# Pair evictions placed ahead of splits, values fetched into their own tiles, an embedding product in two portions, and priority for the first values' weights, in a two-layer mLSTM and retention trunk

## The chip, the cores and the metric

The kernel runs on one core of a Trainium2 chip. Its engines are named as in the profile: PE (TensorE, matrix products; PEld is its loading of weights), DVE (VectorE), ACT (ScalarE), POOL (GpSimd) and SP (SyncE, which here only issues transfers). Each engine works through its own instructions in a fixed order, and an instruction that waits holds up everything behind it on that engine. The metric is device time in microseconds (us); less is better.

## The reference, cut to what matters

The computation is a trunk of two layers over 512 positions of width 1024, in float32. Each layer has an mLSTM branch, a retention branch of four heads, a merge, a feed-forward part of width 4096, and a gated embedding.

```python
for i in range(DEPTH):                       # 2 layers
    h = rmsnorm(x, norm1_g[i])
    z = h @ w_in[i] + b_in[i]                # mLSTM q k v o i f, retention q k v g, two gates
    _, _, mv, mo, mi, mf, rq, rk, rv, rg, gm, gr = split_cols(z)
    qk = jax.nn.silu(causal_conv(z[..., :2 * M_QK], conv_w[i], conv_b[i]))
    hm = mlstm_chunkwise(mq, mk, mv, mi, log_sigmoid(mf))
    y_m = sigmoid(mo) * head_layernorm(hm, m_norm_g[i], M_HEADS)
    rq4, rk4 = rope(rq), rope(rk) * R_DK ** -0.5
    hr = retention_chunkwise(rq4, rk4, rv, log_gamma)      # 4 heads, dk 256, dv 512
    y_r = silu(rg) * head_layernorm(hr, r_norm_g[i], R_HEADS)
    merged = sigmoid(gm) * (y_m @ w_bm[i]) + sigmoid(gr) * (y_r @ w_br[i])
    x = x + merged @ w_out[i]
    h2 = rmsnorm(x, norm2_g[i])
    x = x + square(relu(h2 @ w_ff1[i] + b_ff1[i])) @ w_ff2[i] + b_ff2[i]
    h3 = rmsnorm(x, norm3_g[i])
    x = x + sigmoid(h3 @ w_pe_gate[i]) * (p[i] @ w_pe[i])   # the embedding
return rmsnorm(x, final_g)
```

## The kernel before, in words

**Precision.** Every float32 operand is kept as two tiles, a rounded "hi" and the rest "lo". The function `split` makes them: ACT copies the source into hi (L286), DVE subtracts hi from the source into lo (L287). A product is then three matmuls, hi by hi, hi by lo and lo by hi (L442 to L444 for plain products, L491 to L493 for pairs, L534 to L536 for wide products, L746 to L748 for the first values). So each weight passes ACT and DVE before PE can use it.

**Weights.** All weights are streamed once. SP loads them in the order of a list of units into a few raw buffers `wr`; `prep_next` splits the next piece into `wh` and `wl`, two pieces ahead of the product that uses it. In names such as wh53_C, 53 is the unit and C the piece. A unit of kind T8 or V is one 128x1024 piece of eight blocks; PE is the embedding's weight, in two units.

**Pairs.** Two column tiles of a 1024-deep product form a PAIR, computed by Strassen's method in Winograd's form: seven products P1 to P7 of 12 matmuls (256 wide) where eight would be needed. Its weights are four pieces: A serves P1 and P5, B serves P6 and P2, C serves P3 and P7, D serves P4. Sums of weights for A and C are made in memory by DMAs that POOL issues (L331, tiles s*t1 and s*t3, 1 MB each, paced by the matmuls); two further sums are made on DVE (L421, L424). PE runs P1, P5, then the P4 that the pair before left over (`later`, `flush`), then P6, P2, P3, P7, and leaves its own P4. In the profile a product is told by its PSUM tile and its weights, such as l0r2o1a with wh_A. P1, P6, P7 and P4 add up in one PSUM bank ("a"), P5 and P3 in another ("c"), P2 stands alone ("b"). So each later product in a bank must wait until the earlier sum has been read out ("evicted"). In `pair_tiles` P1 (L548), P5 (L550), P6 (L554) and P4 (L560) are read out by ACT, P2 (L552), P3 (L556) and P7 (L558) by DVE.

**Retention heads.** For head h of layer i the names are l{i}r{h}. `r_qk` makes queries and keys (pairs brq and brk with rotary work on DVE), `r_scores` the scores s and p, `r_attend` the product with the values (tile l{i}r{h}a, read out by ACT L783 as num) and its normalisation: statistics on DVE (L791, L792), two small instructions on POOL (L1086, L1087, tile hv), and a scaling on DVE (L797). `r_out` multiplies by the gate (pairs o0 and o1 of the head). Values are computed for two heads at once: head 0 or 2 is split at once into the value tiles vh and vl, head 1 or 3 is written to memory by POOL (L1166). `rv_load` brings the latter back: POOL issues four transfers of 256 KB into temporary tiles vr (L1197), and each tile is split into vh and vl. There is one set of value tiles per branch, so these may be overwritten only when the head before has been read.

**Feed-forward and embedding.** hid tiles (hh, hl) come from ff1; `ff2(b, p)` are pairs named l{i}o{b}{p}, whose evictions add straight into x on DVE (L1400). The last four are o30 to o33. The embedding's product l{i}pe takes two units of 24 matmuls of 512 columns and reads neither x nor hid; ACT copies its eight tiles (L1450). After o33 the third normalisation n3 feeds the gate product l{i}pg.

**What sets the order.** A scheduler lays out each engine's order when the program is built: it takes ready instructions by priority, which is the order of the code, and its own estimate of when inputs are ready. `tc.high_priority(offset)` makes the instructions inside count as if they were written that many places earlier. On the chip the order is then fixed.

Of the kernel before, what the change touches and what calls it, by code (L numbers as in the profile page):

```python
# [53 lines left out]
LOOK = 2  # L54
WARM = 11
# [95 lines left out]
def unit_list(i):  # L151
# [77 lines left out]
    u.append(("PE", 0))  # L229
    u.append(("PE", 1))  # L230
    pairs(ff_order()[1])
# [4 lines left out]
def build(ctx, tc, ins, out):  # L236
# [153 lines left out]
    def prep_next():  # L390
# [15 lines left out]
        if gates:  # L406
            z = out_[0]
            gp.memset(z.bitcast(F32), 0.0)
            z = z.rearrange("p (k g c) -> p k g c", g=4, c=32)
            split(r[:, 0:64].rearrange("p (k g c) -> p k g c", g=2, c=H), z[:, :, 0:2, 0:H], z[:, :, 2:4, 0:H])  # L410
        elif x == 0:
            for c in halves(n):
                in_order("prep", *split(r[:, c], *[a[:, c] for a in out_]))
        else:
            in_order("prep", *split(r[:, :w], *out_))
# [124 lines left out]

    def pair_tiles(name, act, consume, y=None):
# [4 lines left out]
        def done(x, o):  # L546
            if x == "P1":
# [3 lines left out]
            elif x == "P2":  # L551
                ve.tensor_tensor(y[0][:, b], o, y[0][:, b], OP.add)  # L552
            elif x == "P6":
                ac.activation(y[1][:, b], o, AF.Copy)  # L554
            elif x == "P3":
                ve.tensor_tensor(y[1][:, b], o, y[1][:, b], OP.add)  # L556
            elif x == "P7":
                ve.tensor_tensor(y[1][:, a], o, y[1][:, a], OP.add)  # L558
            else:
                ac.activation(y[0][:, a], o, AF.Copy)  # L560
                consume(y)
# [357 lines left out]
    for i in range(L):  # L919
# [272 lines left out]
        def rv_load(h):  # L1192

            v = value_tiles(f"l{i}r{h}")
            for j in range(NT):
                t = tmp(f"l{i}r{h}vr{j}")
                gp.dma_start(t, rv_dram[i, h // 2, j])  # L1197
                split(t, v[0][j][:, :T], v[1][j][:, :T])
            return v

# [81 lines left out]
        num = r_attend(0, pt, vv)  # L1282
        gs = {}
        r_gates(0, 0, gs)
        vv = rv_load(1)
        pt = r_scores(1, qk)
        yr = acts(cur["br"], f"l{i}yr0")
# [8 lines left out]
        num = r_attend(2, pt, vv)  # L1296
        qk = r_qk(3)
# [5 lines left out]
        vv = rv_load(3)  # L1303
        pt = r_scores(3, qk)
        yr = acts(cur["br"], f"l{i}yr1")
# [137 lines left out]
        for u in range(2):  # L1443
            _, wh, wl = unit("PE")
            for c in range(4):
# [4 lines left out]
                ac.activation(pe[:, 4 * u + c, :], o, AF.Copy)  # L1450
        for _, b, p in rest:
            ff2(b, p)
        flush()
# [216 lines left out]
```

## Time and profile before

| | us |
|---|---|
| median of 3 runs | 2349.16 |
| lowest and highest run | 2348.27, 2350.61 |
| the profiled execution's own time | 2347.49 |
| span of that execution in the trace | 2345.8 |
| PE busy in the span | 2320.2 |
| DVE busy | 1722.9 |
| ACT busy | 1218.9 |
| POOL busy | 245.7 |

The trace belongs to one execution; its times of day count from the start of the span. Matmuls overlap each other, so an instruction's own length (0.28 to 0.39 us) is longer than the distance to the next one (0.12 us at 256 columns, 0.23 us at 512). In timeline rows the columns are start, length, engine, line, operation, output and inputs; the square bracket says how long the engine was idle just before and what ended it. In rows of waits the numbers are the sum, the number of waits and the longest.

### The profile page before, as it was taken

What the parts mean: (1) busy time and instruction counts of PE and PEld (TensorE: products, weight loads), DVE (VectorE), ACT (ScalarE), POOL (GpSimd) and SP (SyncE); (2) the same over time, 40 slices, a digit from 0 to 9 for tenths busy, and PEclk for the clock granted to TensorE, in tenths of its full rate; (3) what the DMA queues carried; (4) which work ended last, traced back from release to release, by engine and by line L of the source; (5) the groups of instructions that cost most, each with busy time, mean ns of one, the idle gap of its engine ahead of it and who ended that gap; (6) DMA issues with size and microseconds to landing.
All of it is one profiled execution on the core that took longest, in us unless ns stands there. A gap on an engine that the chain in (4) does not pass through costs nothing. (4 is left out here: it accounts for less than half of the span.)

```text
span 2345.8 us, 35261 instructions
## 1 busy us (share of the span) xinstructions
PE 2320.2 (99%) x13660; PEld 2056.2 (88%) x13660; DVE 1722.9 (73%) x2658; ACT 1218.9 (52%) x1768; POOL 245.7 (10%) x369
## 2 busy tenths in 40 slices
PE   9999999999999999999999999999999999999998
PEld 7888899898898898899888888998989988998997
DVE  7878767895675577677878787778958656776785
ACT  6656444553554445446557564454536445445454
POOL 3111101100102100000321110000000020000012
PEclk9999999999999999999999999999999999999999
DMA  5666676667578667676775645434343542433431
GB/s 201 187 180 172 218 229 170 205 189 202 168 230 269 195 198 189 199 219 181 206 221 169 182 124 186 136 126 158 108 158 104 166 153 96 130 108 98 132 117 59
DMA packets 146631, 394.89 MB, mean 168 GB/s; under 512 B 15376, under 2 KB 18832, under 8 KB 146464
## 3 DMA queue, kind: packets, MB, share of 16 engines
q1 hardware_dynamic: 99952, 247.77, 32.0%
q0 software_dynamic: 31104, 117.45, 20.4%
q10 hardware_dynamic: 15408, 27.43, 3.3%
q8 instruction: 107, 1.75, 0.3%
q14 instruction: 60, 0.49, 0.1%
HBM read 373.71 MB, written 123.73 MB: 212 GB/s over the span
## 5 line engine op out<-in xcount | busy, mean ns | idle before, releaser
L286 ACT ACTIVATE wh<-wr 128x1024 fp32r<-128x1024 f32 (+1 forms) x223 | 232.2, 1044 | 276.5 <-issue 69.6
L287 DVE TENSOR_TENSOR wl<-wr,wh 128x1024 fp32r<-128x1024 f32 (+1 forms) x221 | 271.9, 1232 | 77.7 <-ACT wh L286 77.5
L286 ACT ACTIVATE wh_B<-wr 128x1024 fp32r<-128x1024 f32 x100 | 105.9, 1059 | 159.2 <-PE l0f L443 8.5
L287 DVE TENSOR_TENSOR wl_B<-wr,wh_B 128x1024 fp32r<-128x1024 f32 x100 | 121.9, 1219 | 32.5 <-ACT wh_B L286 32.3
L286 ACT ACTIVATE wh_D<-wr 128x512 fp32r<-128x512 f32 x76 | 48.0, 632 | 124.9 <-DVE wr L424 65.4
L286 ACT ACTIVATE wh_C<-wr 128x1024 fp32r<-128x1024 f32 x76 | 80.2, 1056 | 61.3 <-issue 9.2
L286 ACT ACTIVATE wh_A<-wr 128x1024 fp32r<-128x1024 f32 x76 | 79.9, 1052 | 54.7 <-PE l1f L443 9.0
L287 DVE TENSOR_TENSOR wl_C<-wr,wh_C 128x1024 fp32r<-128x1024 f32 x76 | 94.3, 1240 | 18.7 <-ACT wh_C L286 18.5
L287 DVE TENSOR_TENSOR wl_A<-wr,wh_A 128x1024 fp32r<-128x1024 f32 x76 | 92.7, 1220 | 17.3 <-ACT wh_A L286 17.3
L442 PE MATMUL l1f<-l1n2h,wh 128*128 128x512 f32 x256 | 99.8, 390 | 0.0
L442 PE MATMUL l0f<-l0n2h,wh 128*128 128x512 f32 x256 | 99.8, 390 | 0.0
L444 PE MATMUL l0f<-l0n2h,wl 128*128 128x512 f32 x256 | 99.7, 389 | 0.0
L444 PE MATMUL l1f<-l1n2h,wl 128*128 128x512 f32 x256 | 99.7, 389 | 0.0
L443 PE MATMUL l1f<-l1n2l,wh 128*128 128x512 f32 x256 | 99.6, 389 | 0.0
L443 PE MATMUL l0f<-l0n2l,wh 128*128 128x512 f32 x256 | 99.6, 389 | 0.0
L287 DVE TENSOR_TENSOR wl_D<-wr,wh_D 128x512 fp32r<-128x512 f32 x76 | 52.4, 689 | 33.2 <-ACT wh_D L286 31.7
L421 DVE TENSOR_TENSOR wr<-wr,wr 128x512 f32<-128x512 f32 x76 | 52.1, 686 | 14.6 <-DMA wr<-wpairs 13.1
L444 PEld LDWEIGHTS l0f<-l0n2h,wl 128*128 128x128 f32 x256 | 48.0, 188 | 10.2
L444 PEld LDWEIGHTS l1f<-l1n2h,wl 128*128 128x128 f32 x256 | 48.1, 188 | 10.1
L443 PEld LDWEIGHTS l1f<-l1n2l,wh 128*128 128x128 f32 x256 | 48.1, 188 | 9.8
L442 PEld LDWEIGHTS l0f<-l0n2h,wh 128*128 128x128 f32 x256 | 48.1, 188 | 9.8
L442 PEld LDWEIGHTS l1f<-l1n2h,wh 128*128 128x128 f32 x256 | 48.1, 188 | 9.7
(5625 smaller groups left out, 8357.9 us busy)
## 6 DMA issues: line engine op xcount, KB each, us to landing
wr<-wstream SPq DMA_DIRECT2D x219, 512.0 KB, 4.2
wr<-wpairs SPq DMA_DIRECT2D x228, 256.0 KB, 2.8
wr<-wwide SPq DMA_DIRECT2D x24, 512.0 KB, 4.0
s0t<-wwide POOLq DMA_DIRECT2D x5, 1024.0 KB, 7.8
s4t<-wwide POOLq DMA_DIRECT2D x5, 1024.0 KB, 9.0
s12t<-wwide POOLq DMA_DIRECT2D x5, 1024.0 KB, 8.1
s16t<-wwide POOLq DMA_DIRECT2D x5, 1024.0 KB, 8.5
s1t<-wpairs POOLq DMA_DIRECT2D x4, 1024.0 KB, 6.7
```

The costliest lines, as they stand in the source:

```text
L286: a = ac.activation(hi_ap, src, AF.Copy)
L287: return a, ve.tensor_sub(lo_ap, src, hi_ap.bitcast(F32))
L421: ve.tensor_tensor(raws[n, "B"][:, Q:], kept.pop((n, "A"))[:, Q:], r[:, :Q], OP.add)
L442: te.matmul(o, sh, mh, start=first, stop=False)
L443: te.matmul(o, sh, ml, start=False, stop=False)
L444: cur["mm"] = te.matmul(o, sl, mh, start=False, stop=last)
```

## The change

It has four parts.

1. In `pair_tiles` every eviction is issued under a priority of 250 places ahead, so the scheduler puts it ahead of splits that were written before it. What follows the last eviction (`consume`) keeps its priority.
2. `rv_load` is taken apart. `rv_fetch` issues the four transfers straight into the lo value tiles, right after the attend of the head before; `rv_split`, after the scores, lets ACT copy lo into hi and DVE subtract hi from lo in place. The four temporary tiles vr are gone.
3. The embedding's two units are parted: unit 0 stays before the last ff2 pairs, unit 1 comes after them, and the P4 that o33 leaves is run in the middle of unit 1 (after its second tile). SP's order of loads moves with it.
4. The splits of the first values' weights (units of kind V below 10, so layer 0 alone) get the priority of 250 places.

```diff
+AHEAD = 250
@@ list of units
     pairs(ff_order()[0])
     u.append(("PE", 0))
+    pairs(ff_order()[1])
     u.append(("PE", 1))
-    pairs(ff_order()[1])
     full("w_pe_gate")
@@ prep_next
         elif x == 0:
-            for c in halves(n):
-                in_order("prep", *split(r[:, c], *[a[:, c] for a in out_]))
+            with tc.high_priority(AHEAD if n < 10 and units[n][0] == "V" else 0):
+                for c in halves(n):
+                    in_order("prep", *split(r[:, c], *[a[:, c] for a in out_]))
@@ pair_tiles
+    def ahead():
+
+        return tc.high_priority(AHEAD)
+
...
         def done(x, o):
+            with ahead():
+                evict(x, o)
+            if x == "P4":
+                consume(y)
+
+        def evict(x, o):
             if x == "P1":
...
             else:
                 ac.activation(y[0][:, a], o, AF.Copy)
-                consume(y)
@@ values of the odd heads
-        def rv_load(h):
+        def rv_fetch(h):
 
             v = value_tiles(f"l{i}r{h}")
             for j in range(NT):
-                t = tmp(f"l{i}r{h}vr{j}")
-                gp.dma_start(t, rv_dram[i, h // 2, j])
-                split(t, v[0][j][:, :T], v[1][j][:, :T])
+                gp.dma_start(v[1][j][:, :T].bitcast(F32), rv_dram[i, h // 2, j])
             return v
+
+        def rv_split(v):
+            for hi, lo in zip(*v):
+                split(lo[:, :T].bitcast(F32), hi[:, :T], lo[:, :T])
@@ the layer
         num = r_attend(0, pt, vv)
+        vv = rv_fetch(1)
         gs = {}
         r_gates(0, 0, gs)
-        vv = rv_load(1)
         pt = r_scores(1, qk)
+        rv_split(vv)
...
         num = r_attend(2, pt, vv)
+        vv = rv_fetch(3)
         qk = r_qk(3)
...
-        vv = rv_load(3)
         pt = r_scores(3, qk)
+        rv_split(vv)
@@ the embedding
-        for u in range(2):
+
+        def embed(u):
             _, wh, wl = unit("PE")
             for c in range(4):
...
                 ac.activation(pe[:, 4 * u + c, :], o, AF.Copy)
+                if c == 1:
+                    flush()
+
+        embed(0)
         for _, b, p in rest:
             ff2(b, p)
-        flush()
+        embed(1)
```

In the changed program line numbers are higher, by 1 at the top and by 10 to 16 further down: L286 and L287 become L287 and L288, L331 becomes L332, the evictions L548 to L560 become L560 to L572, L1086 becomes L1097, L1400 becomes L1415. How the order moved is shown at three places.

The first is POOL in layer 0, around the values of head 3 (l0r3). Tiles s7t to s9t are sums of weights. Before, the end of the sums for s8 and then the fetch into vr:

```order
L331 DMA s8t3_110<-wpairs 256x1024
L331 DMA s8t1_109<-wpairs 256x1024
L331 DMA s8t3_110<-wpairs 256x1024
L1197 DMA l0r3vr0_6030<-rv_spill_83 128x512
L1197 DMA l0r3vr1_6034<-rv_spill_83 128x512
L1197 DMA l0r3vr2_6038<-rv_spill_83 128x512
L1197 DMA l0r3vr3_6042<-rv_spill_83 128x512
L331 DMA s9t1_111<-wpairs 256x1024
```

In the changed program, the same fetch, now into vl:

```order
L332 DMA s7t1_107<-wpairs 256x1024
L1207 DMA l0r3vl0_5465<-rv_spill_83 128x512
L1207 DMA l0r3vl1_5466<-rv_spill_83 128x512
L1207 DMA l0r3vl2_5467<-rv_spill_83 128x512
L1207 DMA l0r3vl3_5468<-rv_spill_83 128x512
L1097 TENSOR_SCALAR l0r2hv_5454<-l0r2mv_5445 128x4
L1098 TENSOR_TENSOR l0r2hv_5454<-l0r2hv_5454,nhalf_89 128x4
L332 DMA s7t3_108<-wpairs 256x1024
```

The fetch moved past five sums of weights (the last of s7 and the four of s8), and now stands ahead of the two small instructions that the normalisation of head 2 needs.

The second is ACT in layer 0, around the first gate pair of head 0 (l0r0o0). Before, with kh the keys of head 1 and num the last read-out of head 0's attend:

```order
L783 ACTIVATE l0r0num_3984<-l0r0a3_4036 128x512
L286 ACTIVATE l0r1kh0_3733<-l0r1brku0_4003 128x512
L548 ACTIVATE l0r0o0y0_4067<-l0r0o0a_4078 128x256
L286 ACTIVATE l0r1kh1_3735<-l0r1brku1_4010 128x512
L550 ACTIVATE l0r0o0y1_4068<-l0r0o0c_4098 128x256
L554 ACTIVATE l0r0o0y1_4068<-l0r0o0a_4078 128x256
L286 ACTIVATE wh52_D_4094<-wr77_3850 128x512
L286 ACTIVATE wh53_A_4112<-wr78_3852 128x1024
L286 ACTIVATE l0r1vh0_4174<-l0r1vr0_4182 128x512
```

In the changed program:

```order
L794 ACTIVATE l0r0num_3984<-l0r0a3_4036 128x512
L287 ACTIVATE l0r1kh1_3735<-l0r1brku1_4010 128x512
L287 ACTIVATE l0r1vh0_4067<-l0r1vl0_4071 128x512
L560 ACTIVATE l0r0o0y0_4079<-l0r0o0a_4090 128x256
L287 ACTIVATE l0r1vh1_4068<-l0r1vl1_4072 128x512
L287 ACTIVATE l0r1vh2_4069<-l0r1vl2_4073 128x512
L287 ACTIVATE l0r1vh3_4070<-l0r1vl3_4074 128x512
L562 ACTIVATE l0r0o0y1_4080<-l0r0o0c_4110 128x256
L566 ACTIVATE l0r0o0y1_4080<-l0r0o0a_4090 128x256
L287 ACTIVATE wh52_D_4106<-wr77_3850 128x512
```

The four copies of head 1's values moved from behind three evictions (P1, P5, P6) to places between the attend and the evictions of P1 and P5.

The third is DVE near the start, around the split of unit 8, the last but one of the first values' weights; the rows between are the work on gates (lower-case g names) and on the convolution (z and cv) of mLSTM head 0. Before:

```order
L287 TENSOR_TENSOR wl7_0_580<-wr7_264,wh7_0_579 128x1024
L853 SCALAR_TENSOR_TENSOR l0glb_471<-ones_r_87,l0glf_469 4x128 x4
L855 SCALAR_TENSOR_TENSOR l0gm_476<-l0glf_469,l0gli_447 4x512
...
L979 TENSOR_TENSOR l0m00cv_495<-l0m00cv_495,l0fix_252 128x3
L978 SCALAR_TENSOR_TENSOR l0m01cv_506<-l0m01z_507,bc_84,l0m01cv_506 128x510
L287 TENSOR_TENSOR wl8_0_610<-wr8_360,wh8_0_609 128x1024
```

In the changed program:

```order
L288 TENSOR_TENSOR wl7_0_580<-wr7_264,wh7_0_579 128x1024
L857 TENSOR_TENSOR l0gd_463<-l0gd_463,l0gu_461 4x512
L858 SCALAR_TENSOR_TENSOR l0gf_446<-l0gf_446,l0gd_463 4x512
L288 TENSOR_TENSOR wl8_0_610<-wr8_360,wh8_0_609 128x1024
L864 SCALAR_TENSOR_TENSOR l0glb_471<-ones_r_87,l0glf_469 4x128 x4
```

The split of unit 8 moved past eight instructions on gates and nine of the convolution (one of each kind of row is shown, or two); those now run behind it.

## The prediction

> **What bounds the kernel now.** I read the page first, then the waits of PE, then the timeline at the waits the change touches.
>
> ```profile
> span 2345.8 us, 35261 instructions
> PE 2320.2 (99%) x13660; PEld 2056.2 (88%) x13660; DVE 1722.9 (73%) x2658; ACT 1218.9 (52%) x1768; POOL 245.7 (10%) x369
> ```
>
> PE is the bound: it is busy for all but 25.6 us, and the change removes no matmul. So it can win only what PE waits, plus what PE loses at a low clock, and it loses by any new wait of PE. The waits of PE (total, number, longest) that stand near the change:
>
> ```profile
> PE l0r2o1a L491 <- ACT wh_A L286: 3.4, 1, 3.4
> PE l1o33a L491 <- DVE l1x L1400: 1.6, 1, 1.6
> PE l0o33a L491 <- DVE l0x L1400: 1.3, 1, 1.3
> PE l0m0vp L747 <- DVE wl L287: 1.3, 1, 1.3
> PE l0r0o0a L491 <- DVE l0r0o0y L558: 1.2, 1, 1.2
> PE l1r0o0a L491 <- DVE l1r0o0y L558: 1.2, 1, 1.2
> PE l0r1brqa L491 <- DVE l0r1brqy L558: 1.0, 1, 1.0
> PE l1r2o0a L491 <- ACT l1r2o0y L548: 0.5, 1, 0.5
> PE l0r2o0a L491 <- ACT l0r2o0y L548: 0.4, 1, 0.4
> PE l1r2o1a L491 <- DVE l1r2o1y L558: 0.3, 1, 0.3
> PE l0r2o1a L491 <- DVE l0r2o1y L558: 0.2, 1, 0.2
> ```
>
> The longest is in layer 0, at the gate pairs of head 2. POOL, ACT and PE there, and the windows of the two stretches behind it and of one in layer 1 (length; busy time of PE, PEld, DVE, ACT, POOL; clock; DMA share; GB/s):
>
> ```profile
> 587.23 0.90 POOL L331 DMA_DIRECT2D s8t<-wpairs  x1 [9.98 <-DMA br_spill<-l0brs]
> 587.88 1.95 POOL L1197 DMA_DIRECT2D l0r3vr<-rv_spill  x3
> 598.58 0.63 ACT L286 ACTIVATE l0r3vh<-l0r3vr 128x512 fp32r<-128x512 f32 x1 [2.83 <-DMA l0r3vr<-rv_spill]
> 602.69 1.04 ACT L286 ACTIVATE wh_A<-wr 128x1024 fp32r<-128x1024 f32 x1
> 603.78 0.58 PE L491 MATMUL l0r2o1a<-l0xnh,wh_A 128*128 128x256 f32 x1 [3.40 <-ACT wh_A L286]
> 602.40:609.20 6.80, 5.06 (x22) 4.77 (x23) 4.96 (x11) 3.99 (x9) 0.00 (x0) 0.50 0.48 172
> 609.20:616.00 6.80, 6.80 (x59) 6.80 (x59) 3.91 (x6) 3.25 (x7) 0.00 (x0) 1.00 0.25 80
> 1563.00:1583.00 20.00, 18.79 (x137) 17.77 (x136) 18.75 (x35) 13.12 (x21) 4.02 (x6) 1.00 0.47 150
> ```
>
> POOL issued three of the four value transfers at 587.88, just behind 1 MB of weight sums. They landed so late that ACT stood idle 2.83 us for the first it came to, and the split of wh_A, behind these copies on ACT, ended at 603.73. PE waited 3.40 us and then ran at half clock for the rest of a 6.80 us stretch.
>
> **The change part by part.** *Fetch of head 3.* In the new order POOL issues it at head 2's attend, some 60 us earlier, and ACT and DVE split the values among the pairs r3brq. Nothing of it stands before wh_A any more, and PE's order there becomes regular again. In layer 0 goes 3.40, the 0.35 and 0.2 that follow it (the rows of 0.4 and 0.2) and the half clock: 5.06 us for 22 matmuls, against 6.80 / 59 = 0.115 each at full clock, is 5.06 - 2.53 = 2.5 lost; a few matmul records may be missing, so 2.4. Sum -6.35, between -3.4 (the clock's loss comes back by another wait) and -6.9. In layer 1 there was no late landing, and the two evictions waited for (0.5 and 0.3) no longer stand behind splits: -0.8, between 0 and -0.8. The cover of the moved fetch is head 3's brq and brk work; what it costs there comes below.
>
> *Embedding in two portions.* 48 matmuls of l0pe:
>
> ```profile
> L442 PE MATMUL l0pe<-l0pth,wh x16: 394/394/397, 1077.3 to 1087.6; 128*128 128x512 f32 x16
> L444 PE MATMUL l0pe<-l0pth,wl x16: 392/392/394, 1077.8 to 1088.1; 128*128 128x512 f32 x16
> 1083.55 1.23 DVE L287 TENSOR_TENSOR l0hl<-l0f33st,l0hh 128x1024 fp32r<-128x1024 f32 x1 [1.13 <-ACT l0hh L286]
> 1088.33 0.28 PE L491 MATMUL l0o30a<-l0hh,wh_A 128*128 128x256 f32 x1
> 1089.39 1.23 DVE L287 TENSOR_TENSOR wl_B<-wr,wh_B 128x1024 fp32r<-128x1024 f32 x1 [2.46 <-ACT wh_B L286]
> 1127.01 1.98 DVE L287 TENSOR_TENSOR wl<-wr,wh 128x1024 fp32r<-128x1024 f32 x1
> 1128.91 0.41 DVE L1400 TENSOR_TENSOR l0x<-l0x,l0o33a 128x256 f32<-128x256 f32 x1
> ```
>
> They start over (1088.1 - 1077.3) / 47 = 0.23 us apart. At o33 the eviction of P7 stood behind a split of the next weights on DVE (1127.01 to 1128.9), and P4 waited 1.3 us (1.6 in layer 1). Twelve embedding matmuls, 2.8 us, now lie there and hide it: -2.9 in both layers. But o30 loses 24 matmuls of cover and would start 5.5 us earlier, at 1082.8, while the last hid tile is split only until 1084.8. P1 doesn't read that part; P6 comes two products (2.8 us) later, at 1085.7, and its third matmul needs wl_B. DVE can do wl_B only after 1084.8, one eviction (0.33) and 1.2 for itself, so by 1086.3: a wait of 0.4, up to 1.0 with the L421 sum that moved ahead of the hid split. I take 0.5 a layer: -2.9 + 1.0 = -1.9, between -2.9 and 0.
>
> *Priority for the first values' weights.* wl of unit 8 moved past 17 DVE instructions:
>
> ```profile
> 50.68 1.22 DVE L287 TENSOR_TENSOR wl<-wr,wh 128x1024 fp32r<-128x1024 f32 x1
> 69.90 0.50 PE L442 MATMUL l0m0s<-l0m0qh,l0m0kh 128*128 128x512 f32 x1
> ```
>
> PE waited 1.3 us for it. Of what now runs later, PE first needs the convolution's queries and keys, at 69.90, and it reads 18 us of other products before. -1.3, between 0 (another product waits instead) and -1.4.
>
> *Evictions ahead, at r0o0.* This part meets the moved fetch of head 1 on ACT:
>
> ```profile
> L444 PE MATMUL l0r0a<-l0r0vh,l0r0pl x10: 389/389/398, 395.0 to 402.9; 128*128 128x512 f32 x10
> DMA to landing us min/median/max: 2.9/3.4/3.7
> 404.84 0.39 ACT L548 ACTIVATE l0r0o0y<-l0r0o0a 128x256 f32<-128x256 f32 x1 [0.24 <-PE l0r0o0a L493]
> 406.49 0.37 ACT L550 ACTIVATE l0r0o0y<-l0r0o0c 128x256 f32<-128x256 f32 x1
> 410.31 1.92 DVE L797 TENSOR_SCALAR l0r0num<-l0r0num,l0r0mv,l0r0hv 128x512 f32<-128x512 f32 x4 [1.26 <-POOL l0r0hv L1087]
> 415.67 0.42 DVE L558 TENSOR_TENSOR l0r0o0y<-l0r0o0a,l0r0o0y 128x256 f32<-128x256 f32 x1
> ```
>
> (The second row is the landing of l0r1vr.) The first fetch can be issued when the attend has read vl0 for the last time, about 2 us before its end at 403.2, the last one at that end. With 3.4 us to land they arrive at about 404.6 to 406.6. ACT then copies vh0, evicts P1, copies vh1 to vh3 and evicts P5: the last copy starts at about 406.9 and the eviction ends at about 407.9, where it ended at 406.9 before. PE's new order brings P3 forward (two matmuls each of P6 and P2 and three of the scores lie between), to 407.2, so P3 waits about 0.7. P7's eviction is ahead of the splits now, but on DVE still behind the scaling L797, which waits for POOL's hv. hv comes behind the four fetches, so L797 ends near 411.6, and behind it come L424, vl0 and wl_D at 0.6 each and P2's and P3's evictions at 0.33, until 414.1; P7's eviction ends at 414.5, and PE is there at about 414.2. So 1.2 goes and about 1.2 comes (0.7, 0.3 and small shifts): 0 a layer, between -1.2 and +1.5.
>
> *The fetch of head 3, at r3brq.*
>
> ```profile
> 530.14 0.39 ACT L548 ACTIVATE l0r3brqy<-l0r3brqa 128x256 f32<-128x256 f32 x1 [0.71 <-PE l0r3brqa L493]
> ```
>
> ACT had spare time here. Now vh0 and vh1 stand ahead of P1's eviction. The attend ends at 528.5, so vl1 lands near 530.5 and its copy ends near 531.1; P1's eviction moves from 530.5 to 531.5, and P6, due at 531.36, waits about 0.2 to 0.3. +0.3 a layer, between 0 and +1.3: +0.6.
>
> *The rest.* r1brq's wait (1.0) is one for P7's eviction behind a sum that awaited a load; order there is unchanged: 0. The other evictions of pairs move by a place or two among work that nobody waits for, hidden by the DVE's 27% and ACT's 48% of idle time; without that cover each would cost its 0.4 us.
>
> Sum: -6.35 - 0.8 - 1.9 - 1.3 + 0 + 0.6 = -9.75 us. The profiled execution took 2347.49 us, so 2337.7; the median of the runs stands 1.67 above it, so **2339.4 us**.
>
> For a POOL transfer the Trainium skill (DMA: Bandwidth & Descriptors, section "Anatomy of one DMA — SWDGE (gpsimd) path") fits 2.0 us plus the bytes at 436 GB/s. My estimate from it, if the four share that rate as one megabyte, is 4.4 us for the last, later than the row's 2.9 to 3.7. By it P5's eviction at r0o0 and P1's at r3brq come up to 0.7 us later in both layers, and the sum is about -7. The row was measured with the weight stream running, so I go by the row.
>
> **The rivals.** *Slower: the copies of values hold up evictions.* At four places (r0o0 and r3brq, two layers) ACT now waits for a DMA ahead of an eviction that PE needs. Each us of landing beyond 3.4 is one us of PE's time at each. The sum is used up at 3.4 + 9.75 / 4 = 5.8 us; at 7 us it is +14.4, so 2354. For it:
>
> ```profile
> DMA to landing us min/median/max: 4.4/11.1/12.1
> 383.81 0.57 POOL L331 DMA_DIRECT2D s6t<-wpairs  x1 [7.57 <-PE l0r1brqa L493]
> 510.34 0.95 POOL L331 DMA_DIRECT2D s7t<-wpairs  x1 [14.89 <-PE l0r2s L444]
> ```
>
> The first row is l0r3vr behind the 1 MB sum, so such landings exist. Against it: the other two rows are the sums that stand ahead of the fetches in the new order of layer 0, issued 15 us or more before the attends end (403 and 528); and the fetch of head 1 took 3.7 at most. 0.12.
>
> *The gains are given back.* Embedding 0 instead of -1.9 and a full us at each of the four places: -6.35 - 0.8 - 1.3 + 4 = -4.5, 2344.7. DVE's 2.46 us of idle time at 1089.39 is just the slack that the earlier start takes away. 0.2.
>
> *More gain.* The evictions go first and no copy holds them: -6.35 - 0.8 - 2.9 - 1.3 - 2.4 = -13.75, 2335.4. The new ACT order speaks against it. 0.1.
>
> *The half clock stays.* In the layer 1 window a wait of 1.2 us left the clock at 1.00, so the new waits of about 1 us shouldn't halve it; if one grows to 3.4, it costs 2.4 more. That is inside the first rival. The Trainium skill (TensorE: Matmul & The Clock Gate, Part 1) has a free-running window of 3413 ns, so by it a wait of that length may or may not halve the clock; one row here can't show that.
>
> **How the numbers follow.** The forecast has the rest, 0.58, with its own range of 2335.5 to 2343.5. The range must reach into the rival that gives back and the start of the slower one: 2334 to 2349. A measurement of this kernel can tell 0.2% (4.7 us) from no change. Faster: the forecast, more gain and half of the given back, 0.77. Same: the other half, 0.1. Slower: 0.13, the first rival and something unseen.
>
> **What would show it.** Right: no wait at l0r2o1a, clock 1.00 around it, none at o33a and m0vp; waits of under 1 us at r0o0c (for L562) and r0o0a (for L570), of 0.3 at r3brqa (for L560) and 0.5 at o30a (for wl_B). Wrong: ACT idle for 2 us or more before vh of r1 or r3; a wait over 1 us at o30 to o32; an hv that comes after 411 in layer 0.

## The result, and the profile after

| | before | after |
|---|---|---|
| median of 6 runs, us | 2349.66 | 2339.36 |
| lowest and highest, us | 2348.27, 2350.89 | 2338.39, 2342.72 |
| the profiled execution's own time, us | 2347.49 | 2342.72 |
| its span, us | 2345.8 | 2341.0 |

The ratio is 0.9961 (95% interval 0.9951 to 0.9971): the changed kernel is 0.3 to 0.5% faster. The forecast was 2339.4. That agreement is partly luck. The profiled execution of the change is the longest of its six runs, 3.4 us above their median, while that of before lay 2.2 us under its median here. So the two traces differ by 4.8 us and the medians by 10.3, and the terms of the sum have to be tested one by one.

The page of the change, its span and busy times:

```profile
span 2341.0 us, 35229 instructions
PE 2320.0 (99%) x13660; PEld 2055.5 (88%) x13660; DVE 1722.4 (74%) x2658; ACT 1223.2 (52%) x1771; POOL 243.5 (10%) x369
```

PE is still the bound and is as busy as before; what went is waiting (25.6 us of the span without PE became 21.0). The waits of PE in the change (total, number, longest):

```profile
PE l0bgm L446 <- DVE wl L288: 1.6, 1, 1.6
...
PE l0r0o0c L493 <- ACT l0r0o0y L562: 0.8, 1, 0.8
...
PE l1r0o0c L493 <- ACT l1r0o0y L562: 0.7, 1, 0.7
PE l1r3brqa L493 <- ACT l1r3brqy L560: 0.6, 1, 0.6
...
PE l0r2o1a L493 <- DVE l0r2o1y L570: 0.4, 1, 0.4
PE l1r2o1a L493 <- DVE l1r2o1y L570: 0.3, 1, 0.3
...
PE l0o30a L495 <- DVE wl_B L288: 0.3, 1, 0.3
PE l1o30a L495 <- DVE wl_B L288: 0.3, 1, 0.3
...
PE l1r0o0a L493 <- DVE l1r0o0y L570: 0.2, 1, 0.2
```

The wait of 3.4 us for wh_A at l0r2o1a is gone, as are those at o33a and at l0m0vp. The short waits for P7's eviction at r2o1a (L570) are still there. New are the waits at r0o0c, l1r3brqa and o30a, and one at l0bgm that no step of the prediction names. In the change l0r2o1a starts at 608.52, and the window behind it (length; busy time of PE, PEld, DVE, ACT, POOL; clock; DMA share; GB/s) has full clock:

```profile
608.80:615.60 6.80, 6.80 (x60) 6.80 (x59) 4.30 (x7) 4.89 (x9) 0.00 (x0) 1.00 0.28 83
```

Before, PE made 22 matmuls in the 6.80 us around this start, with 1.4 us of the wait among them and the clock at 0.50; now it makes 60.

Where the time went is best seen from the start of the same PE tile in both traces. A difference that grows is a loss.

| first matmul of | before, us | after, us | difference | change since the row above | predicted |
|---|---|---|---|---|---|
| l0n1ss (first normalisation) | 21.54 | 23.23 | +1.69 | +1.69 | 0 |
| l0gtp (behind the first values) | 57.41 | 57.45 | +0.04 | -1.65 | -1.3 |
| l0m1a | 142.76 | 146.35 | +3.59 | +3.55 | 0 |
| l0r2va (behind head 0's o0, o1) | 437.00 | 440.83 | +3.83 | +0.24 | 0 |
| l0r2o0a (behind r3brq) | 595.92 | 599.98 | +4.06 | +0.23 | +0.3 |
| l0r3o0a | 631.46 | 629.13 | -2.33 | -6.39 | -6.35 |
| l0pe | 1077.33 | 1074.91 | -2.42 | -0.09 | 0 |
| l0n3rp (behind the embedding and o33) | 1141.86 | 1137.74 | -4.12 | -1.70 | -0.8 |
| l1r3brqa (behind head 0's o0, o1) | 1692.07 | 1687.59 | -4.48 | -0.36 | 0 |
| l1r2o0a (behind r3brq) | 1759.48 | 1755.85 | -3.63 | +0.85 | +0.3 |
| l1r3o0a | 1789.44 | 1785.00 | -4.44 | -0.81 | -0.8 |
| l1pe | 2233.26 | 2229.89 | -3.37 | +1.07 | 0 |
| l1n3rp | 2297.89 | 2293.13 | -4.76 | -1.39 | -1.1 |

(The predicted -1.9 of the embedding is shared out by its layers: waits of 1.3 and 1.6 gone, 0.5 come in each.) Three rows stand out: the loss of 3.55 between l0gtp and l0m1a, the 1.69 at the start and the 1.07 late in layer 1. The first has a visible cause. The bias of the first values, tile l0m0bv (128x512), is loaded by SP; DVE adds it. In the timeline of before:

```profile
20.41 31.89 SPq L386 DMA_DIRECT2D wr<-wstream  x5
55.33 0.33 SPq L733 DMA_DIRECT2D l0m0bv<-bv  x1
57.85 0.99 POOL L331 DMA_DIRECT2D s0t<-wwide  x1 [10.62 <-PE l0m0vp L748]
61.49 1.40 DVE L716 SCALAR_TENSOR_TENSOR l0m0v<-l0m0vp,l0n1rc,l0m0bv 128x512 f32<-128x512 f32 x2
```

and of the change:

```profile
21.96 34.92 SPq L387 DMA_DIRECT2D wr<-wstream  x7
57.88 0.98 POOL L332 DMA_DIRECT2D s0t<-wwide  x1 [7.89 <-PE l0m0vp L759]
58.51 0.33 SPq L744 DMA_DIRECT2D l0m0bv<-bv  x1
66.89 0.75 DVE L727 SCALAR_TENSOR_TENSOR l0m0v<-l0m0vp,l0n1rc,l0m0bv 128x512 f32<-128x512 f32 x1 [4.35 <-DMA l0m0bv<-bv]
```

With part 4 two more weight loads stand ahead of the bias in SP's queue (from 20 us on, seven instead of five). It left 3.2 us later, and just behind POOL's 1 MB sum s0t instead of ahead of it. DVE, with all its convolution and splitting work queued behind the addition, stood idle for 4.35 us until the bias was there, 8.4 us after its issue (66.89 - 58.51). At 108 us DVE still ran the same work 4 us later than before. PE felt it at l0bgm (1.6 us) and in smaller waits up to 143 us. The split that l0bgm needs, in the trace of before and of the change, and the matmul that waited for it:

```profile
108.17 1.19 DVE L287 TENSOR_TENSOR wl<-wr,wh 128x1024 fp32r<-128x1024 f32 x1
...
112.18 1.19 DVE L288 TENSOR_TENSOR wl<-wr,wh 128x1024 fp32r<-128x1024 f32 x1
113.42 0.50 PE L446 MATMUL l0bgm<-l0n1h,wl 128*128 128x512 f32 x1 [1.65 <-DVE wl L288]
```

### The profile page after: what moved, and what is told of

The parts are those of the page before. It is cut to its first block, busy times and chain, and to the rows that moved or that the text cites. A ratio compares the mean times of both kernels' runs of the same rounds, so it can differ in the third digit from the quotient of the medians.

```text
span 2341.0 us, 35229 instructions
## 1 busy us (share of the span) xinstructions
PE 2320.0 (99%) x13660; PEld 2055.5 (88%) x13660; DVE 1722.4 (74%) x2658; ACT 1223.2 (52%) x1771; POOL 243.5 (10%) x369
## 3 DMA queue, kind: packets, MB, share of 16 engines
q8 instruction: 107, 1.75, 0.3%
## 4 chain that ended last, share of the span: by engine, by line
PE 87%; DVE 5%; issue 4%; DMA 2%; ACT 1%; POOL 0%; DVEq 0%; ACTq 0%; POOLq 0%; SPq 0%
PE l1f L444 2%; PE l0f L444 2%; PE l0f L445 2%; PE l1f L445 2%; PE l1f L446 2%; PE l0f L446 2%; PE l0br L444 1%; PE l1br L444 1%; PE l0br L446 1%; PE l1br L445 1%; PE l1br L446 1%; PE l0br L445 1%; DMA wr<-wpairs 1%; PE l0pg L444 1%; PE l1bm L444 1%
## 5 line engine op out<-in xcount | busy, mean ns | idle before, releaser
L287 ACT ACTIVATE wh<-wr 128x1024 fp32r<-128x1024 f32 (+1 forms) x223 | 231.2, 1043 | 282.3 <-issue 71.6
L288 DVE TENSOR_TENSOR wl<-wr,wh 128x1024 fp32r<-128x1024 f32 (+1 forms) x221 | 272.2, 1233 | 76.5 <-ACT wh L287 74.9
L287 ACT ACTIVATE wh_B<-wr 128x1024 fp32r<-128x1024 f32 x100 | 105.9, 1059 | 153.4 <-PE l0bm L445 13.1
L288 DVE TENSOR_TENSOR wl_B<-wr,wh_B 128x1024 fp32r<-128x1024 f32 x100 | 122.0, 1220 | 27.2 <-ACT wh_B L287 27.1
L287 ACT ACTIVATE wh_D<-wr 128x512 fp32r<-128x512 f32 x76 | 47.9, 631 | 127.5 <-DVE wr L426 67.6
L287 ACT ACTIVATE wh_C<-wr 128x1024 fp32r<-128x1024 f32 x76 | 80.3, 1056 | 63.6 <-issue 10.5
L288 DVE TENSOR_TENSOR wl_A<-wr,wh_A 128x1024 fp32r<-128x1024 f32 x76 | 92.8, 1221 | 20.2 <-ACT wh_A L287 20.2
L288 DVE TENSOR_TENSOR wl_C<-wr,wh_C 128x1024 fp32r<-128x1024 f32 x76 | 94.3, 1241 | 15.7 <-ACT wh_C L287 15.3
L287 ACT ACTIVATE wh_A<-wr 128x1024 fp32r<-128x1024 f32 x76 | 80.0, 1052 | 46.1 <-PE l1f L445 6.7
L288 DVE TENSOR_TENSOR wl_D<-wr,wh_D 128x512 fp32r<-128x512 f32 x76 | 52.4, 690 | 36.9 <-ACT wh_D L287 35.7
```

Of the source, the lines that this page charges most:

```text
L287: a = ac.activation(hi_ap, src, AF.Copy)
L288: return a, ve.tensor_sub(lo_ap, src, hi_ap.bitcast(F32))
```

## The experiments

The ratio is always to the kernel before, run on the same chip in the same group of runs. In the group of the last row that kernel itself spread from 2344.27 to 2351.30.

| kernel | median us (runs) | before, us | ratio, 95% interval |
|---|---|---|---|
| the change again | 2341.53 (5) | 2349.19 | 0.9967 (0.9954 to 0.9979) |
| the change without part 4 | 2339.83 (5) | 2349.19 | 0.9960 (0.9948 to 0.9973) |
| part 4 alone | 2351.85 (11) | 2349.19 | 1.0011 (1.0002 to 1.0020) |
| part 2 alone (fetch) | 2344.67 (11) | 2349.19 | 0.9981 (0.9972 to 0.9990) |
| part 1 alone (evictions) | 2348.07 (11) | 2349.79 | 0.9995 (0.9986 to 1.0003) |
| part 3 alone (embedding) | 2345.74 (11) | 2349.79 | 0.9985 (0.9976 to 0.9994) |
| before, head 3's transfers issued by ACT | 2351.52 (10) | 2349.79 | 1.0012 (1.0003 to 1.0021) |
| without part 4, copies behind P6 | 2337.32 (5) | 2349.79 | 0.9951 (0.9939 to 0.9964) |
| the change, bias loaded early | 2337.83 (5) | 2349.66 | 0.9950 (0.9938 to 0.9963) |
| all parts, bias early, copies behind P6 | 2337.28 (5) | 2349.66 | 0.9950 (0.9937 to 0.9964) |
| before, sums paced later | 2343.19 (9) | 2349.66 | 0.9973 (0.9963 to 0.9982) |
| the change, sums paced later | 2336.93 (5) | 2347.58 | 0.9952 (0.9938 to 0.9966) |

### Part 4, away and alone

**The change again.**

> The changed kernel once more, with a second profile. In the first profile (an execution of 2342.7 us) DVE waited 4.35 us for the bias of the first values (tile l0m0bv), and PE lost about 3.5 us between 70 and 130 us; other executions took 2338.4 to 2339.5. My theory: the late bias is what divides them. If this profile's execution takes about 2338.7, the wait for l0m0bv is under 1 us and PE loses under 1 us between 70 and 130. If it takes about 2342.7, the wait is there again. Rival: the wait is in both kinds of execution, and the difference lies elsewhere (the start, or the pace of the matmuls).

Its profiled execution took 2342.19 us. DVE waited 4.0 us for the bias again and PE 1.6 us at l0bgm. The late bias is thus no accident of one execution. But this execution is a long one too, so whether the late bias divides the long executions from the short ones was not tested.

**Without part 4.**

```diff
-            with tc.high_priority(AHEAD if n < 10 and units[n][0] == "V" else 0):
+            with tc.high_priority(0):
```

> The change without its fourth part (priority for the first values' weights). The prediction has that part at -1.3, so this takes 2340.7. Theory from the first profile: the part wins 1.66 at l0m0vp and gives back up to 3.5 by the late bias, so without it the wait of 1.3 at l0m0vp is back, the bias lands in time, and the time is 2340 +- 0.7 in every execution, with none near 2342.7. If the executions still fall into two groups 4 us apart, the late bias isn't the cause.

In its trace the bias, issued at 55.4 us, landed in 3.2 us, and between l0n1ss and l0m1a nothing was lost against before (the two starts differ by 0.00 and +0.13 us). The wait that part 4 removes was there again, 1.4 us at l0m0vp. The eleven runs of the change have a median of 2339.86, and these five 2339.83: by the medians part 4 is worth nothing in this company. None of the five came near 2342.7, but they spread wider than expected, from 2338.00 to 2340.78.

**Part 4 alone**, on the kernel before:

```diff
+AHEAD = 250
...
-            for c in halves(n):
-                in_order("prep", *split(r[:, c], *[a[:, c] for a in out_]))
+            with tc.high_priority(AHEAD if n < 10 and units[n][0] == "V" else 0):
+                for c in halves(n):
+                    in_order("prep", *split(r[:, c], *[a[:, c] for a in out_]))
```

> The kernel before with the fourth part alone. By the prediction -1.3 us. By the first profile of the change: -1.7 at l0m0vp, and up to +3.5 from a bias that DVE waits for, so between -1.7 and +1.9, and the wait of PE at l0m0vp gone in any case.

Alone it makes the kernel slower, by 0.02 to 0.2%. The rows of the tile l0m0bv in its trace, the load (first and last start stand at the row's end) and what DVE waited for:

```profile
L735 SPq DMA_DIRECT2D l0m0bv<-bv x1: 328/328/328, 57.3 to 57.3; - x1
its engine sat idle before it (us, times) until:
  DMA l0m0bv<-bv: 3.9, 1
```

The bias left at 57.3, 0.7 us behind the sum s0t at 56.6, and came 8 us later. The wait at l0m0vp was gone, 1.65 us by l0gtp, and 1.71 came back by l0m1a: nothing is won. The median rose by 2.66. The one trace that there is is 2.2 us longer than that of before, elsewhere: 0.4 us at the start, 0.6 at l0r2o1a, 0.5 at l0o12a and 1.1 from l1o00a to l1o10a. The last stands in every trace but that of before and isn't part 4's; whether part 4 causes any of the others is open.

### The other parts, one at a time

**Part 2 alone.**

```diff
         num = r_attend(0, pt, vv)
+        vv = rv_fetch(1)
         gs = {}
         r_gates(0, 0, gs)
-        vv = rv_load(1)
         pt = r_scores(1, qk)
+        rv_split(vv)
...
         num = r_attend(2, pt, vv)
+        vv = rv_fetch(3)
         qk = r_qk(3)
...
-        vv = rv_load(3)
         pt = r_scores(3, qk)
+        rv_split(vv)
```

> The kernel before with the second part alone (values fetched into their own tiles, earlier). By the prediction: -6.35 at l0r2o1a with its half clock, and some waits at r0o0 and r3brqa; the waits of r2 in layer 1 (0.5 and 0.3) may stay: -5 to -6.5. Rival (the wait at l0r2o1a comes of ACT's order, which the first part changes, and not of the late landing): the wait of 3.4 stays and the gain is under 2 us.

The wait of 3.4 us was gone, and the stretch from l0r2o0a to l0r3o0a took 6.4 us less than before, as in the change. But without part 1 the copies cost more at head 0. Its waits of PE:

```profile
PE l1r0o0a L491 <- DVE l1r0o0y L558: 1.8, 1, 1.8
PE l0r0o0a L491 <- DVE l0r0o0y L558: 1.8, 1, 1.8
...
PE l1r3brqa L491 <- ACT l1r3brqy L548: 0.7, 1, 0.7
```

1.8 instead of 1.2 us: P7's eviction came later here. From l0r0o0a to l0r2va 2.1 us were lost, in layer 1 0.6. A gain of 5 to 6.5 us had been expected; the median gained 4.5, and these losses alone are larger than the gap. So the parts 1 and 2 help each other, and that was only half foreseen: the prediction had the 1.2 us go by part 1 and others come by part 2.

**Part 1 alone.**

```diff
...
         def done(x, o):
+            with ahead():
+                evict(x, o)
+            if x == "P4":
+                consume(y)
```

> The kernel before with the first part alone (evictions ahead of splits). By the prediction's reasoning the moved fetch is what takes this part's gain at r0o0; alone it should win there: 1.2 in each layer, and up to 0.4 to 0.8 at head 2, so -2.4 to -3.5, while the 3.4 us at l0r2o1a stay, since ACT's copies of head 3 still stand ahead of wh_A. Rival: P7's eviction is held by the scaling L797 that waits for POOL, not by splits; then the wait at r0o0 stays and the gain is under 1 us.

```profile
PE l0r2o1a L492 <- ACT wh_A L287: 3.5, 1, 3.5
...
PE l1r0o0a L492 <- DVE l1r0o0y L569: 0.2, 1, 0.2
PE l0r0o0a L492 <- DVE l0r0o0y L569: 0.2, 1, 0.2
```

At r0o0a the 1.2 us became 0.2 in both layers, with no wait in the rows for r0o0c. The starts show less: from l0r0o0a to l0r2va PE won 0.49 us and in layer 1 0.48, not 1.0 each. The 3.4 us at l0r2o1a stayed, as expected, but the gain of 2.4 to 3.5 us that had been expected didn't come: it is unclear by the interval whether the median (-1.7) is a gain at all.

**Part 3 alone.**

```diff
+    pairs(ff_order()[1])
     u.append(("PE", 1))
-    pairs(ff_order()[1])
...
-        for u in range(2):
+        def embed(u):
...
+                if c == 1:
+                    flush()
+        embed(0)
         for _, b, p in rest:
             ff2(b, p)
-        flush()
+        embed(1)
```

> The kernel before with the third part alone. Prediction: -1.9 (2.9 gained at o33, 0.5 lost at o30 in each layer). By the profiles of the change the loss at o30 is 0.3 to 0.4 a layer and the gain larger: -3.1. Rival (DVE has no room, the earlier start is paid for later in o31 and o32): 0.

```profile
PE l0o30a L493 <- DVE wl_B L287: 0.3, 1, 0.3
...
PE l1o30a L493 <- DVE wl_B L287: 0.3, 1, 0.3
```

From l0pe to l0n3rp it won 1.25 us and in layer 1 1.75, so 3.0; by the medians 4.05. The prediction said 1.9, and the expectation before this run 3.1.

### Why head 3's values came late

**The transfers issued by ACT**, to see whether POOL's queue, behind its own 1 MB sum, made them late:

```diff
-                gp.dma_start(t, rv_dram[i, h // 2, j])
+                (nc.scalar if h == 3 else gp).dma_start(t, rv_dram[i, h // 2, j])
```

> The kernel before, but the four transfers of head 3's values are issued by ACT instead of POOL, at the same place in the program and into the same tiles. If they landed late because they queue behind the 1 MB sum on POOL, they now land in 3 to 4 us, the wait at l0r2o1a falls below 0.5 us, and the time falls by about 6 us. If they landed late because the sum and the weight stream fill the DMA engines whoever issues, they still take 8 us or more, the wait stays near 3 us and the time within 1 us.

It became slower. The transfers were issued between 593.7 and 600.4 us. The timeline of ACT, and PE's wait:

```profile
595.41 1.11 ACTq L1197 DMA_DIRECT2D l0r3vr<-rv_spill  x2
600.31 0.63 ACT L286 ACTIVATE l0r3vh<-l0r3vr 128x512 fp32r<-128x512 f32 x1 [5.37 <-DMA l0r3vr<-rv_spill]
```

```profile
PE l0r2o1a L491 <- ACT wh_A L286: 6.5, 1, 6.5
```

In this trace the one landing that is shown took 6.6 us, neither the 3 to 4 of the one theory nor the 8 or more of the other, and ACT stood still for 5.4. Another queue at this place is no remedy. But ACT issued the first transfer 5.8 us later than POOL had (593.68 against 587.88), so the run doesn't show how a transfer from another queue at POOL's time would have landed. The windows of this kernel:

```profile
590.00:595.00 5.00, 5.00 (x24) 4.15 (x23) 1.48 (x3) 1.54 (x2) 0.00 (x0) 1.00 0.97 180
595.00:600.00 5.00, 5.00 (x41) 5.00 (x40) 2.10 (x3) 0.00 (x0) 0.58 (x1) 1.00 1.04 331
600.00:605.00 5.00, 1.74 (x15) 1.53 (x13) 1.92 (x3) 1.59 (x3) 0.00 (x0) 1.00 0.96 381
```

The DMA share is 0.96 to 1.04 while the transfers are on their way: here too they meet full DMA engines.

**The sums paced later**, in the kernel before:

```diff
-    at = {"unit": 0, "credit": -12.0, ...}
+    at = {"unit": 0, "credit": -16.0, ...}
```

> The kernel before, with every weight sum of POOL paced about 5.5 us later, so that the fetch of head 3's values in layer 0 no longer stands right behind a 1 MB sum but between two, with the one ahead 5 to 6 us older. If the neighbouring sum is what makes them land late: landing of 3 to 6 us instead of 11 to 12, the wait at l0r2o1a under 1 us, no stretch of half clock there, and -4 to -6 us. Rival (the weight stream alone fills the DMA engines there): landing of 8 us or more and the wait stays.

POOL's timeline, and the landing of head 3's values:

```profile
582.29 0.93 POOL L331 DMA_DIRECT2D s8t<-wpairs  x1 [10.32 <-PE l0br L444]
582.98 1.94 POOL L1197 DMA_DIRECT2D l0r3vr<-rv_spill  x3
591.83 0.55 POOL L1197 DMA_DIRECT2D l0r3vr<-rv_spill  x1 [6.92 <-DMA br_spill<-l0brs]
```

```profile
DMA to landing us min/median/max: 6.4/9.3/9.9
```

The edit didn't do what was intended: the transfers are still right behind a sum, and they still land late after their issue (9.3 us in the middle), so this run doesn't decide whether the sum or the weight stream holds them up. But they are issued 4.9 us earlier, and ACT reads them from 596.2 on without waiting. That alone removed the wait at l0r2o1a and the low clock, 5.25 us between l0r2o0a and l0r3o0a, and 6.5 us of the median. What costs is when the values arrive against wh_A's turn on ACT; for that the fetch needn't move to another place in the program.

### Which parts can be mended

**Copies behind P6.** In the change without part 4, ACT's copies of the fetched values are ordered behind the evictions of P1, P5 and P6 of r0o0 and r3brq:

```diff
-                ac.activation(y[1][:, b], o, AF.Copy)
+                cur[name] = ac.activation(y[1][:, b], o, AF.Copy)
...
-                split(lo[:, :T].bitcast(F32), hi[:, :T], lo[:, :T])
+                a, _ = split(lo[:, :T].bitcast(F32), hi[:, :T], lo[:, :T])
+                tc.add_manual_dep(a.ins, cur[behind].ins.name, ORDER, reason="evictions first")
...
```

> The change without its fourth part, and with ACT's copies of the fetched values placed behind the evictions of P1, P5 and P6 of the pair beside them (r0o0 for head 1, r3brq for head 3). My theory: the waits at r0o0c (0.8 and 0.9) and r3brqa (0.5 in layer 1) come of the copies standing ahead, so they go and the time is 2337.6 (2.2 below the change without the fourth part). Rival: DVE's chain (scaling behind hv, then evictions) is the next to end, the wait moves to P4 of r0o0, and the time is 2339 to 2340.

The waits at r0o0c and r3brqa were gone, and l1r3brq lost nothing (-0.01 against +0.77 in the same kernel without the ordering). A new wait stood at r0o0a:

```profile
PE l0r0o0a L493 <- ACT wh_A L287: 0.8, 1, 0.8
PE l1r0o0a L493 <- ACT wh_A L287: 0.8, 1, 0.8
```

The copies now delay the split of the next weights instead of an eviction. 0.8 replaces 0.8 at r0o0; the gain of 2.5 us in the median over the same kernel without the ordering is more than the 0.8 that the two traces show at these places, and the intervals overlap.

**Bias early.** The change, with the bias in a tile of its own that is free at that time, loaded some ten loads earlier:

```diff
-        bvt = tmp(f"{nm}bv")
-        nc.sync.dma_start(bvt, bv_ap)
+        if nm == "l0m0":
+            bvt = cur["br"].tile([P, T], F32, name="l0m0bv", tag="dec")
+        else:
+            bvt = tmp(f"{nm}bv")
+        with tc.high_priority(60 if nm == "l0m0" else 0):
+            nc.sync.dma_start(bvt, bv_ap)
```

> The change, but the bias of the first values has a tile of its own that is free from the start, and its load is issued some ten loads earlier on SP, well ahead of the 1 MB sum that POOL issues near 58 us. My theory of the fourth part: the bias lands late because it is issued next to that sum, DVE then waits 4 us for it and PE loses 3.0 to 3.5 us between 70 and 130 us. So DVE's wait for l0m0bv is gone, PE loses under 1 us there, and the time is about 2337.5, some 2.5 below the change. Rival (the priority itself put work behind, the bias only made it seen): PE still loses 2 us or more there and the time stays at 2339.5 to 2340.5.

```profile
21.90 0.42 SPq L748 DMA_DIRECT2D l0m0bv<-bv  x1
...
57.24 0.99 POOL L332 DMA_DIRECT2D s0t<-wwide  x1 [7.85 <-PE l0m0vp L763]
59.01 0.74 DVE L727 SCALAR_TENSOR_TENSOR l0m0v<-l0m0vp,l0n1rc,l0m0bv 128x512 f32<-128x512 f32 x1
```

DVE no longer waited. From l0gtp to l0m1a the trace loses nothing (-0.62 us against before at both), where the change loses 3.55, and the gain of 1.66 at l0m0vp stays. All five runs (2336.62 to 2338.09) lie below all eleven of the change (2338.39 to 2343.02).

**The change with the sums paced later**: one number altered (the credit, -12 to -16, as above), the bias left where the change puts it.

> The change with one number altered: the credit from which POOL's 1 MB sums of weights are paced goes from -12 to -16, so that each comes some 6 us later in PE's work. In the change the bias of the first values (l0m0bv) was issued at 58.5 us, 0.6 us behind a sum at 57.9, and DVE had to wait for it until 66.9. With the later pacing that sum starts near 65, where it stood in the kernel before with the same number. Theory (the 1 MB sum makes the bias late): the bias, issued near 58.5, lands within 4.5 us, DVE waits less than 1 us for it, nothing is lost between 70 and 143 us, the wait at l0m0vp stays gone, and the median comes to about 2337.5 (2336 to 2339). Rival (the place in SP's queue makes it late, behind two loads of weights, whatever POOL does): DVE waits about 4 us again, PE loses some 3.5 us by 143 us, and the median stays at 2339 to 2342. Both theories leave the stretches behind that as in the change, unless a later sum meets a fetch of values, which would show as ACT idle for 2 us or more before vh of head 1 or 3.

```profile
20.58 34.76 SPq L387 DMA_DIRECT2D wr<-wstream  x7
56.96 0.33 SPq L744 DMA_DIRECT2D l0m0bv<-bv  x1
60.91 0.74 DVE L727 SCALAR_TENSOR_TENSOR l0m0v<-l0m0vp,l0n1rc,l0m0bv 128x512 f32<-128x512 f32 x1
62.91 0.98 POOL L332 DMA_DIRECT2D s0t<-wwide  x1 [11.53 <-PE l0bgm L446]
```

The bias is in the same place of SP's queue as in the change, behind seven loads from 20 us on. With the sum 6 us behind it, DVE had it without idling within 3.95 us of its issue (60.91 - 56.96), and nothing was lost up to l0m1a. That decides between the two theories: the 1 MB sum makes the bias late, not the place in SP's queue. The median is the expected one, but the later sums moved more than the bias: from l0r2va to l0r3brqa this trace loses 1.6 us that the change doesn't, and it wins 2.0 us from l0o12a to l0pe, where the change wins 0.1. So the gain in the median can't all be put down to the bias.

**All together** (all four parts, the bias early and the copies behind P6; the edits are the two above).

> All four parts, with the early bias and with the copies of the fetched values behind the evictions of P1, P5 and P6. If both mends add up: 2337.3 of the copies behind P6 without the fourth part, less 1.4 for l0m0vp, so 2336. If the start pays for the fourth part (1.4 to 2.0 us later at the first norm in both profiles of the change), 2337 to 2338.

2337.28 us. This version, the copies behind P6, the bias early and the change with the later sums stand at ratios of 0.9950 to 0.9952 and can't be told apart; by the ratios each is some 2 to 3 us ahead of the change (0.9961). So of the two mends one is enough, and together they don't add up: 2337.83 became 2337.28 where the copies alone had gained 2.5. Why they don't is open.

## Why the prediction was right, and where it was not

**Fetch of head 3: right in place and size, with some luck.** -6.35 was predicted in layer 0 and -6.39 came, with no wait for wh_A and full clock; -0.8 and -0.81 in layer 1. But the waits for P7's eviction at r2o1a that the term counted as gone (0.2 and 0.3) stayed (0.4 and 0.3), and other steps made up for them: in layer 1 the wait of 0.5 at r2o0a had cost 0.64 by the starts of its matmuls. The rest is not traced. The two lower bounds of the term (the clock's loss comes back, the covers fail) didn't come about. The landings bear out the choice of row. Those of the fetched values in layer 0, heads 1 and 3:

```profile
DMA to landing us min/median/max: 3.0/3.4/3.8
...
DMA to landing us min/median/max: 3.0/3.4/4.0
```

They are 3.4 us in the middle, as the old fetch of head 1. The estimate that the prediction drew from the Trainium skill (DMA: Bandwidth & Descriptors, section "Anatomy of one DMA — SWDGE (gpsimd) path") was 4.4 us for the last of the four; here it took 3.8 and 4.0, between that and the row.

**Evictions ahead, at r0o0: right.** 0 was predicted, 1.2 going and as much coming by 0.7 at P3 and 0.3 at P4. The profile has 0.8 and 0.7 at r0o0c for L562 and 0.2 or less at r0o0a, and from r0o0a to r2va the two layers changed by -0.08 and -0.12 (the table's rows, +0.24 and -0.36, hold much else). With part 1 alone the same stretches won 0.49 and 0.48: the difference is the price of the fetched values' copies. That is the rival "copies hold up evictions", in its small form: it needed 5.8 us of landing to decide, and 4.0 was the most.

**The fetch of head 3, at r3brq: mechanism right, size uneven.** +0.3 a layer was predicted; +0.23 came in layer 0 and +0.85 in layer 1, inside its range of 0 to 1.3. The wait is the one named, for L560's eviction behind the copies, and with the copies ordered behind the evictions it is gone. But it differs from one execution to the next: the second profile of the change lost 0.18 and 0.13, with no such wait, and the one with the bias early lost 0.81 in layer 0 and 0.24 in layer 1.

**Embedding in two portions: mechanism right, mis-sized.** -1.9 was predicted (2.9 won at o33, 0.5 a layer lost at o30). -3.1 came in the change (-1.70 and -1.39) and -3.0 alone. The waits at o33a went and those at o30a for wl_B came, but of 0.3 us each, not 0.5. And the loss at o33 was larger than its wait's row: in the trace of before the first matmul behind it started 1.74 us after its neighbour in layer 0 and 1.98 in layer 1, where the neighbours of 512 columns stand 0.23 apart. So 1.5 and 1.75 were lost, 0.35 more than the rows' 1.3 and 1.6. The term by these numbers is -3.25 + 0.6 = -2.65; the remaining 0.4 lies in smaller steps that I didn't trace.

**Priority for the first values' weights: wrong, sign and all.** The step said: "Of what now runs later, PE first needs the convolution's queries and keys, at 69.90, and it reads 18 us of other products before. -1.3, between 0 (another product waits instead) and -1.4." The wait of 1.3 went, as said. What the step overlooked is a DMA: it counted the 17 DVE instructions that wl passes, and not that the bias's load moves behind two more weight loads in SP's queue and, by that, behind POOL's sum. In the two profiled executions of the change this cost 3.55 and 4.2 us up to l0m1a, and 1.7 alone, so the term was +1.9, +2.7 and 0.1 there; by the medians it is 0 in company (2339.86 against 2339.83) and +0.5 to +4.7 alone. With the bias out of the way it is a gain.

**The total was right because errors cancel.** Against the sum of -9.75 the medians moved by -10.3. Part 4 gave 1.3 or more less than forecast, the embedding 1.1 more. The addition of 1.67 us for the distance of the profile to the median was a property of one execution of before, not of the kernel: the change's profiled execution lies above its median. In before's trace the stretch from l1o00a to l1o10a took 82.45 us, and in the other profiles, also of kernels that don't touch it, 83.55; that is the 1.1 us lost late in layer 1. Why that one was quicker I can't tell. Nor can the +1.69 us at the start be explained: no part touches it, it was 2.2 in the second profile of the change, 1.0 with the bias early and 0.0 in the change with the later sums. With single profiles and a spread of 4.6 us over the change's eleven runs, what differs between its own executions stays open; that the bias lands earlier in the shorter ones would fit, but no profile of a short one exists.

**The rivals.** Of the signs of being wrong that the prediction names, none appeared: ACT idled 0.5 to 1.2 us in all for each head's fetched values, no wait of PE at o30 to o32 was over 0.3 us, and hv was ready at 413.5, which is 409.6 by the times of before, since r0o0 started 3.9 us later. "The gains are given back" (2344.7) and "slower" (2354) didn't happen. "More gain" (2335.4) was wrong for the change, since copies do hold the evictions; with them ordered behind, the kernel comes within 2 us of it. "The half clock stays" was no danger in the change, whose longest wait at these places is 0.8 us; but the threshold that it named, 3.4 us, was too high, as the last section shows.

## What to carry to other kernels

When a step is moved, list the small loads that ride in the same queues, and see which big transfer each will then stand beside: here a 256 KB bias (128x512 float32) beside a 1 MB sum ate what a priority had won, and loading it early, or the sum later, gave it back. A moved load brings its consumer's place with it: put what waits for a DMA behind the instructions that others wait for on that engine. And test a change of several parts one by one, even when the total fits.

## What was not expected of the hardware

**A small transfer right behind a 1 MB one lands late, from SP as from POOL.** From SP the bias took 3.2 to 3.5 us where it was issued ahead of the sum or well clear of it, and came 8 us or more after its issue where it followed 0.6 or 0.7 us behind. The values of head 3, issued by POOL right behind a sum, took 11.1 us in the middle in the kernel before and 9.3 with the later sums; issued by ACT 5 us behind a sum, with the DMA share at 1, the one landing shown took 6.6. Where no sum stood right ahead of them, the values took 3.4 in the middle.

**The clock can halve after a wait of 1.8 us, or not.** With part 2 alone PE waited 1.8 us at r0o0a in both layers. In layer 0 the clock fell:

```profile
418.00:420.00 2.00, 1.82 (x13) 1.85 (x14) 2.00 (x6) 0.72 (x1) 0.00 (x0) 0.86 0.65 193
420.00:422.00 2.00, 2.00 (x12) 2.00 (x11) 1.25 (x4) 1.90 (x5) 0.24 (x1) 0.50 0.83 332
422.00:424.00 2.00, 2.00 (x15) 2.00 (x15) 2.00 (x6) 0.91 (x4) 0.41 (x1) 0.78 0.49 86
...
1577.00:1579.00 2.00, 1.45 (x12) 1.48 (x13) 2.00 (x6) 0.72 (x1) 0.00 (x0) 1.00 0.47 113
1579.00:1581.00 2.00, 2.00 (x19) 2.00 (x19) 2.00 (x5) 1.75 (x4) 0.00 (x0) 1.00 1.01 408
```

In layer 1, with the same wait, it did not. The low stretch lasted 3.4 us (0.14, 0.50 and 0.22 short of full clock, doubled, times 2 us) and cost 1.5 us: 2.1 were lost in layer 0 from l0r0o0a to l0r2va, 0.6 in layer 1. After the wait of 3.4 us in the kernel before it lasted 6.8, twice that, and after one of 3.5 us with part 1 alone 3.4 again. This agrees with the free-running window of 3413 ns that the Trainium skill describes (TensorE: Matmul & The Clock Gate, Part 1): the low stretches are one or two windows long. That the outcome depends on where in the window the wait falls would fit too, but no run here varied only that. From 30 us on and up to the last normalisation, in all the profiles here, waits of PE up to 1.65 us left the clock at 1.00, and those of 3.4 us and more never did. In the last normalisation, where waits of 1.0, 0.4 and 1.0 us stand close together, the clock was halved to the end (0.50 from 2331.6 us on in the change).
